# Two mixers: the products of a head's outputs grouped by kind, and attention's products ordered by tile before head

## The chip, the core and the metric

The kernel runs on one core of a Trainium2 chip, in float32. The metric is the device time of one execution in microseconds (us): the median of three runs is 1829.69 us (1829.17 to 1829.71).

## What is computed

512 tokens of width 1024 go through two blocks. The first is a mixer (a gated linear recurrence called hgrn2 beside a spatial gate), a mixture of 32 experts and a small per-layer embedding. The second is a mixer (stick-breaking attention beside gated linear attention) and an MLP. The change touches the recurrence of the first mixer and the attention of the second:

```python
def hgrn2_branch(q, f_raw, i_in, og, lb, norm_g):        # 4 heads, key and value 128 wide
    C = HG_CHUNK                                         # 64 tokens, 8 chunks
    ...
    att = jnp.einsum('bcthk,bcshk->bchts', q_dec, k_inv)
    att = jnp.where(mask, att, jnp.zeros_like(att))
    o_intra = jnp.einsum('bchts,bcshv->bcthv', att, v)
    dS = jnp.einsum('bcshk,bcshv->bchkv', k_end, v)
    ...                                                  # S = decay * S + dS, from chunk to chunk
    o_inter = jnp.einsum('bcthk,cbhkv->bcthv', q_dec, s_starts)
    o = (o_intra + o_inter).reshape(B, S, HG_HEADS, HG_VAL)
    o = o * lax.rsqrt(jnp.mean(o * o, axis=-1, keepdims=True) + EPS)
    ...

def stick_breaking_attention(q, k, v):                   # 8 heads of 64
    for start in range(0, s_len, Q_BLOCK):
        ...
        z = jnp.einsum('bhtd,bhsd->bhts', q[:, :, start:end], kb) * scale
        log_beta = jax.nn.log_sigmoid(z)
        log_fail = jnp.where(past, log_beta - z, 0.0)
        later = lax.cumsum(log_fail, axis=3, reverse=True) - log_fail
        w = jnp.where(past, jnp.exp(log_beta + later), 0.0)
        outs.append(jnp.einsum('bhts,bhsd->bhtd', w, vb))
```

## The kernel before

Every engine has an instruction list of its own; a scheduler decides the order of the lists from the order of the code, its priorities and the free buffers, and semaphores join them. So an edit of one loop can move other instructions too. The big projections go through `acc` rows (lines 268 to 270): a weight block is split into a high and a low part (`whi` on ACT, line 165; `wlo` on DVE, line 167), and each 128x512 output takes 24 matmuls.

**hgrn** (line 462 on) works on two heads at a time (`hp`), each head `m` of the pair in this order. Scores `pat` (line 581) are 8 products, one for each chunk of 64 tokens; DVE masks them into `att` (line 583). The states' increments `pds` (line 591) are 7 products of 64 rows, chunk c reading the array's half `i = c % 2` and writing one of two banks; DVE adds them up into the states `hS` (lines 597 and 600). The outputs `po` are 15 products in one bank: for each chunk the product of `att` and the values (line 608, 64 rows by 64 columns) and, from the second chunk on, the product of the decayed query and the state before it (line 611, 128 rows by 64 columns), one behind the other. Even chunks write the lower 64 partitions of `po`, odd ones the upper. ACT squares `po`, GpSimd takes the root (`hst`), DVE scales (`hy`, line 623) and PE transposes the result into `pyb` (line 627). PSUM has 4 banks of kind `acc`, 2 of kind `tr` (transposes) and 2 of kind `m` (`misc`: `pat`, `pds`, `po`) here. The projection of the output gate (`proj_tm` with `eg`) stands behind the first head's outputs in the code.

**sticks** (line 1386 on) handles the 8 heads in 4 pairs, a pair on the two halves of 64 rows, and each pair in three groups of key tiles: tiles 2 and 3 together, tile 1, tile 0. For a group, PE computes the scores `z` (line 1464), 256 and 128 columns for each head in the first group, 384 in the second and 512 in the third. ACT and DVE make softplus values of them (`se`, `sp`), PE adds the running sums to the same banks (lines 1491 and 1494), ACT takes the exponent `sw` (line 1498), GpSimd masks it, and PE multiplies it by the values into `po` (line 1505; the code's `v` products, 64 output partitions for each head). Between the groups a fixed number of `acc` outputs, called fills (24 rows each), are called from the table `FILL`, 11 in all:

```python
FILL = ((1, 0, 1), (1, 0, 1), (1, 0, 1), (3, 1, 1))
        ctx.enter_context(N.banks(acc=1, po=1, pz=3))
```

With one `acc` bank a fill can't begin before ACT has copied out the one before (line 1400 for a query, line 1405 for a key).

Of the kernel before, what the change touches and what calls it, by code (L numbers as in the profile page):

```python
# [18 lines left out]
P = 128  # L19
T = 512  # L20
NT = T // P
# [440 lines left out]
def hgrn(N, a, w_in, hT, yb):  # L462
    nc = N.nc
    C = 64
    with N.pool("hg") as hg:
# [9 lines left out]
        att = []  # L475
# [49 lines left out]
        for hp in range(2):  # L525
            wf = N.wtile(w_in[:, 1536 + hp * 256:1536 + (hp + 1) * 256], KD, 256)
            k_, eb_, qd_, ki_, ke_ = [], [], [], [], []
            tables = N.exp_ln()
            for m in range(2):
                h = 2 * hp + m  # L530
                p = N.acc("pf")
                N.fm_acc(p, wf, m, hT, KD)

                k, s = N.tmp("hk"), N.tmp("hf")
                nc.vector.tensor_scalar(k, p, -87.0, None, op0=OP.max)
                with N.tc.issue_after(tables):
                    nc.scalar.activation(s, k, AF.Exp, scale=-1.0)
                l = N.tmp("hl")
                nc.scalar.activation(l, s, AF.Ln, bias=1.0)
                nc.scalar.activation(s, s, AF.Ln, bias=1.0, scale=lb[:, 20 + h:21 + h])  # L540
                nc.vector.tensor_tensor(s, s, l, op=OP.subtract)
                nc.vector.tensor_tensor(k, k, l, op=OP.add)
                nc.scalar.activation(k, k, AF.Exp, scale=-1.0)
                k1 = lb[:, 24 + h:25 + h]
                b = N.tmp("hb")
                nc.vector.tensor_tensor_scan(b, rst, s, 0.0, op0=OP.mult, op1=OP.add)
                eb = hg.tile([P, T], F32, tag="heb", bufs=2, name="heb")
                nc.scalar.activation(eb, b, AF.Exp)
                nb = N.tmp("hnb")
                nc.scalar.activation(nb, b, AF.Exp, scale=-1.0)  # L550
                ki = hg.tile([P, T], F32, tag="hki", bufs=2, name="hki")
                nc.vector.scalar_tensor_tensor(ki, k, k1, nb, op0=OP.mult, op1=OP.mult)
                b3 = b.rearrange("p (c t) -> p c t", t=C)
                d = N.tmp("hd")
                nc.vector.tensor_tensor(d.rearrange("p (c t) -> p c t", t=C), b3[:, :, C - 1:C].to_broadcast([P, 8, C]),
                                        b3, op=OP.subtract)
                nc.scalar.activation(d, d, AF.Exp)
                nc.vector.scalar_tensor_tensor(d, k, k1, d, op0=OP.mult, op1=OP.mult)
                pt = N.trp("pke")
                for t in range(NT):  # L560
                    nc.tensor.transpose(pt[:, t * P:(t + 1) * P], d[:, t * P:(t + 1) * P], N.ident)
                ke = hg.tile([P, T], F32, tag="hke", bufs=2, name="hke")
                nc.scalar.activation(ke, pt, AF.Copy)
                eb_.append(eb); ki_.append(ki); ke_.append(ke)
            wq = N.wtile(w_in[:, 1024 + hp * 256:1024 + (hp + 1) * 256], KD, 256)
            for m in range(2):
                p = N.acc("pq")
                N.fm_acc(p, wq, m, hT, KD)
                s = N.th1(p, "hq")
                nc.vector.scalar_tensor_tensor(s, s, 1.0, p, op0=OP.add, op1=OP.mult)  # L570
                qd = hg.tile([P, T], F32, tag="hqd", bufs=2, name="hqd")
                nc.vector.scalar_tensor_tensor(qd, s, 0.5, eb_[m], op0=OP.mult, op1=OP.mult)
                qd_.append(qd)

            for m in range(2):
                h = 2 * hp + m
                p = N.misc("pat")
                for j in range(NT):
                    for i in range(2):
                        c = slice((2 * j + i) * C, (2 * j + i + 1) * C)  # L580
                        nc.tensor.matmul(p[i * 64:(i + 1) * 64, j * C:(j + 1) * C], lhsT=ki_[m][:, c], rhs=qd_[m][:, c],
                                         start=True, stop=True)
                nc.vector.copy_predicated(att[m], cm[:, None, :].to_broadcast([P, 4, 64]),
                                          p[:, :256].rearrange("p (j t) -> p j t", j=4))

                S = hg.tile([P, 7, P], F32, tag="hS", bufs=2, name="hS")
                pd = [N.misc("pds0"), N.misc("pds1")]
                for c in range(7):
                    j, i = divmod(c, 2)
                    r = slice(i * 64, (i + 1) * 64)  # L590
                    nc.tensor.matmul(pd[i][:, j * P:(j + 1) * P], lhsT=ke_[m][r, j * P:(j + 1) * P],
                                     rhs=vv[r, j, h * P:(h + 1) * P], start=True, stop=True)
                for c in range(7):
                    j, i = divmod(c, 2)
                    dsl = pd[i][:, j * P:(j + 1) * P]
                    if c == 0:
                        nc.vector.tensor_copy(S[:, 0, :], dsl)
                    else:
                        e = (c + 1) * C - 1
                        nc.vector.scalar_tensor_tensor(S[:, c, :], S[:, c - 1, :], eb_[m][:, e:e + 1], dsl,  # L600
                                                       op0=OP.mult, op1=OP.add)
                po = N.misc("po")
                for j in range(NT):
                    for i in range(2):
                        c = 2 * j + i
                        r = slice(i * 64, (i + 1) * 64)
                        o = po[r, j * P:(j + 1) * P]
                        nc.tensor.matmul(o, lhsT=att[m][r, j, :], rhs=vv[r, j, h * P:(h + 1) * P],
                                         start=True, stop=(c == 0))
                        if c > 0:  # L610
                            nc.tensor.matmul(o, lhsT=qd_[m][:, c * C:(c + 1) * C], rhs=S[:, c - 1, :],
                                             start=False, stop=True)
                st = hg.tile([P, 12], F32, tag="hst", bufs=4, name="hst")
                jk = hg.tile([P, P], F32, tag="jk2", bufs=2, name="jk2")
                for j in range(NT):
                    nc.scalar.activation(jk, po[:, j * P:(j + 1) * P], AF.Square, accum_out=st[:, j:j + 1])
                nc.vector.tensor_scalar(st[:, 4:8], st[:, 0:4], 1.0 / P, EPS, op0=OP.mult, op1=OP.add)
                N.rpow(st[:, 8:12], st[:, 4:8])
                if hp == 0 and m == 0:
                    N.proj_tm(w_in, 2560, hT, eg)  # L620
                y = hg.tile([P, NT, P], F32, tag="hy", bufs=2, name="hy")
                for j in range(NT):
                    nc.vector.scalar_tensor_tensor(y[:, j, :], po[:, j * P:(j + 1) * P], st[:, 8 + j:9 + j],
                                                   G[:, j, h * P:(h + 1) * P], op0=OP.mult, op1=OP.mult)
                pt = N.trp("pyb")
                for j in range(NT):
                    nc.tensor.transpose(pt[:, j * P:(j + 1) * P], y[:, j, :], N.ident)
                N.split(yb[0][:, h, :], yb[1][:, h, :], pt)
# [757 lines left out]
def sticks(N, a, w_in, hT, osb, gv, low, fq, bk, lead):  # L1386
# [3 lines left out]
    with N.pool("sb") as sb, ExitStack() as ctx:  # L1390
# [63 lines left out]
        def pair(c):  # L1454
            po = prev = None
            for tiles in ((2, 3), (1,), (0,)):
# [1 line left out]
                nd, n = len(tiles), sum(T - i * P for i in tiles)  # L1458
                n0 = T - tiles[0] * P
                z = N.bank("pz", "pz", 2)[:, :, :n]  # L1460
                for h in range(2):
                    r, c0 = slice(h * 64, (h + 1) * 64), 0
                    for i in tiles:
                        nc.tensor.matmul(z[:, h, c0:c0 + T - i * P], lhsT=k[c][r, i * P:(i + 1) * P], rhs=q[c][r, i * P:],
                                         start=c0 == 0, stop=True, skip_group_check=True)
                        c0 += T - i * P
                e = sb.tile([P, 2, T], F32, tag="se", bufs=3, name="se")[:, :, :n]
                nc.scalar.activation(e, z, AF.Abs)
# [20 lines left out]
                for h in range(2):  # L1489
# [3 lines left out]
                    for x in range(2):  # L1493
# [4 lines left out]
                nc.scalar.activation(w, z, AF.Exp)  # L1498
                nc.gpsimd.affine_select(diag(w), diag(w), pattern=[[0, 2], [0, nd], [1, P]] if nd == 2 else [[0, 2], [1, P]],
                                        compare_op=OP.is_gt, fill=0.0, base=0, channel_multiplier=-1)  # L1500
                for h in range(2):
                    c1 = n
                    for i in reversed(tiles):
                        c0 = c1 - (T - i * P)
                        nc.tensor.matmul(po[h * 64:(h + 1) * 64, i * P:],  # L1505
                                         lhsT=v[:, i, (2 * c + h) * 64:(2 * c + h + 1) * 64], rhs=w[:, h, c0:c1],
                                         start=(i == NT - 1), stop=(i == 0), skip_group_check=True)
                        c1 = c0
                prev = e[:, :, :n0]
                for _ in range(FILL[c][tiles[0]]):  # L1510
                    next(fill, 0)
# [262 lines left out]
```

## Time and profile before

| what | value |
|---|---|
| median of three runs | 1829.69 us |
| profiled execution | 1830.18 us, of which the span of its instructions is 1828.5 us |
| mean granted TensorE clock | 0.999 of full speed |
| busy | PE 98%, DVE 47%, ACT 32%, POOL 4% of the span |
| first mixer's recurrence | about 60 to 160 us of the span |
| experts' weights arriving at the highest rate | about 410 to 870 us |
| second mixer's attention | about 980 to 1092 us |

PE is TensorE's matmuls, DVE is VectorE, ACT is ScalarE, POOL is GpSimd. A float32 matmul of two plain operands shows as two passes, so 8 such products are a row "x16". In a row of the timeline the first number is the start, the second the time from the first start to the modelled end of the last instruction in it; the next row often starts some 0.07 us before that end, since matmuls are pipelined.

### The profile page before, as it was taken

What the parts mean: (1) busy time and instruction counts of PE and PEld (TensorE: products, weight loads), DVE (VectorE), ACT (ScalarE), POOL (GpSimd) and SP (SyncE); (2) the same over time, 40 slices, a digit from 0 to 9 for tenths busy, and PEclk for the clock granted to TensorE, in tenths of its full rate; (3) what the DMA queues carried; (4) which work ended last, traced back from release to release, by engine and by line L of the source; (5) the groups of instructions that cost most, each with busy time, mean ns of one, the idle gap of its engine ahead of it and who ended that gap; (6) DMA issues with size and microseconds to landing.
All of it is one profiled execution on the core that took longest, in us unless ns stands there. A gap on an engine that the chain in (4) does not pass through costs nothing.

```text
span 1828.5 us, 20908 instructions
## 1 busy us (share of the span) xinstructions
PE 1793.8 (98%) x8425; PEld 1240.1 (68%) x8425; DVE 857.1 (47%) x1620; ACT 586.7 (32%) x953; POOL 76.0 (4%) x136
## 2 busy tenths in 40 slices
PE   7999999999999999999999999999999999999998
PEld 5777888864443444443677668787888888888886
DVE  6565433365545445324764557555224443333333
ACT  6453322322111112111755652424223432222221
POOL 1001000100000000000020010000000000000000
PEclk9999999999999999999999999999999999999999
DMA  5122223979999997999312021212233222332221
GB/s 191 47 92 90 78 93 97 354 258 424 423 423 423 423 409 303 424 423 374 131 36 91 24 73 46 92 36 81 82 103 130 87 72 94 96 104 99 92 92 46
DMA packets 117888, 322.60 MB, mean 176 GB/s; under 512 B 8797, under 2 KB 69393, under 8 KB 93720
## 3 DMA queue, kind: packets, MB, share of 16 engines
q1 hardware_dynamic: 115192, 315.46, 45.7%
q0 software_dynamic: 2016, 3.64, 0.5%
q10 hardware_dynamic: 576, 2.10, 0.3%
q8 instruction: 68, 1.11, 0.3%
q14 instruction: 36, 0.29, 0.0%
HBM read 320.68 MB, written 4.19 MB: 178 GB/s over the span
## 4 chain that ended last, share of the span: by engine, by line
PE 46%; issue 3%; ACT 2%; DVE 1%; POOL 1%; DMA 0%; POOLq 0%; DVEq 0%; ACTq 0%
PE acc L268 7%; PE acc L269 7%; PE acc L270 7%; PE pf L270 3%; PE pf L269 3%; PE pf L268 3%; PE pg L270 2%; PE pg L268 2%; PE pg L269 2%; PE psc L1605 2%; PE pu L270 1%; PE pu L268 1%; PE pu L269 1%; PE pa L1090 1%; PE po L1505 1%
## 5 line engine op out<-in xcount | busy, mean ns | idle before, releaser
L167 DVE TENSOR_TENSOR wlo<-wraw,whi 128x1024 fp32r<-128x1024 f32 (+2 forms) x165 | 226.5, 1384 | 350.9 <-PE pg L269 107.6
L165 ACT ACTIVATE whi<-wraw 128x1024 fp32r<-128x1024 f32 (+2 forms) x169 | 193.3, 1165 | 246.6 <-DMA wraw<-in_w_ff_dram 121.4
L268 PE MATMUL acc<-wh,whi 128*128 128x512 f32 (+1 forms) x448 | 170.7, 381 | 1.7 <-ACT fq L1442 1.0
L269 PE MATMUL acc<-wh,whi 128*128 128x512 f32 (+1 forms) x448 | 170.4, 380 | 0.0
L270 PE MATMUL acc<-wh,wlo 128*128 128x512 f32 (+1 forms) x448 | 169.9, 379 | 0.0
L268 PE MATMUL acc<-whi,wh 128*128 128x512 f32 x288 | 116.2, 404 | 0.6 <-ACT wh L165 0.4
L270 PE MATMUL acc<-whi,wh 128*128 128x512 f32 x288 | 114.9, 401 | 0.9 <-DVE wh L169 0.9
L269 PE MATMUL acc<-wlo,wh 128*128 128x512 f32 x288 | 114.9, 400 | 0.2 <-POOL wlo L167 0.2
L269 PE MATMUL pg<-wh,whi 128*128 128x512 f32 x256 | 101.5, 397 | 0.0
L268 PE MATMUL pg<-wh,whi 128*128 128x512 f32 x256 | 101.3, 396 | 0.0
L270 PE MATMUL pg<-wh,wlo 128*128 128x512 f32 x256 | 101.1, 395 | 0.0
L268 PE MATMUL pf<-whi,jh 128*128 128x512 f32 x256 | 101.1, 395 | 0.0
L269 PE MATMUL pf<-wlo,jh 128*128 128x512 f32 x256 | 101.1, 395 | 0.0
L270 PE MATMUL pf<-whi,jl 128*128 128x512 f32 x256 | 101.1, 395 | 0.0
L268 PEld LDWEIGHTS acc<-wh,whi 128*128 128x128 f32 x448 | 84.5, 189 | 21.5 <-issue 1.5
L269 PEld LDWEIGHTS acc<-wh,whi 128*128 128x128 f32 x448 | 84.5, 189 | 18.0 <-issue 1.8
L270 PEld LDWEIGHTS acc<-wh,wlo 128*128 128x128 f32 x448 | 84.5, 189 | 16.5
L1104 DVE TENSOR_TENSOR X<-pc,X 128x512 f32<-128x512 f32 x128 | 80.6, 684 | 15.2 <-PE pc L1102 14.3
L1090 PE MATMUL pa<-ww,wm 128*64 128x512 f32 x176 | 80.8, 599 | 0.3 <-PEq L803 0.3
L1091 PE MATMUL pa<-ww,wm 128*64 128x512 f32 x168 | 77.3, 599 | 0.0
L1102 PEld LDWEIGHTS pc<-y,OT 128*128 128x128 f32 x256 | 44.6, 188 | 41.7 <-issue 24.1
L1102 PE MATMUL pc<-y,OT 128*128 128x512 f32 x256 | 71.0, 411 | 0.3 <-DVE X L1104 0.2
(472 smaller groups left out, 3454.5 us busy)
## 6 DMA issues: line engine op xcount, KB each, us to landing
ww<-in_w_dram SPq DMA_DIRECT2D x71, 1024.0 KB
wraw<-in_w_in_dram SPq DMA_DIRECT2D x44, 1024.0 KB
wr<-in_w_dram SPq DMA_DIRECT2D x34, 1024.0 KB
wm<-in_w_dram SPq DMA_DIRECT2D x33, 1024.0 KB
wraw<-in_w_ff_dram SPq DMA_DIRECT2D x32, 1024.0 KB
wh<-in_w_dram SPq DMA_DIRECT2D x31, 1024.0 KB
we<-in_w_dram SPq DMA_DIRECT2D x23, 1024.0 KB
wraw<-in_w_out_dram SPq DMA_DIRECT2D x8, 1024.0 KB
```

The lines of the kernel that those rows point to most:

```text
L165: nc.scalar.activation(hi, src, AF.Copy, scale=scale)
L167: (pool or nc.vector).tensor_tensor(lo, src, f32v(hi), op=OP.subtract)
L268: mm(out, lhsT=lh, rhs=rh, start=start, stop=False, **kw)
L269: mm(out, lhsT=lh, rhs=rl, start=False, stop=False, **kw)
L270: mm(out, lhsT=ll, rhs=rh, start=False, stop=stop, **kw)
L1090: nc.tensor.matmul(p[0:64], lhsT=x.xT[:, kk, :64], rhs=wt[0][:, k, :], start=kk == 0, stop=kk == 7)
L1091: x.ups.append(nc.tensor.matmul(p[64:128], lhsT=x.xT[:, kk, 64:], rhs=wt[1][:, k, :], start=kk == 0, stop=kk == 7).ins)
L1102: nc.tensor.matmul(pc, lhsT=OT[:, t * P:(t + 1) * P], rhs=y[i], start=i == 0, stop=i == 1)
L1104: nc.vector.tensor_tensor(x, pc, x, op=OP.add)
L1505: nc.tensor.matmul(po[h * 64:(h + 1) * 64, i * P:], lhsT=v[:, i, (2 * c + h) * 64:(2 * c + h + 1) * 64], rhs=w[:, h, c0:c1], start=(i == N ...
L1605: nc.tensor.matmul(pl[:, cs], lhsT=fk[:, m, cs], rhs=fq[:, m, cs], start=True, stop=True)
```

## The change

In hgrn the scores `pat` go to a bank of kind `tr`. The states of both heads of a pair are computed ahead of the outputs of either. The output gate's projection stands between the two (for the first pair). A head's outputs are now all 8 products of `att` first and then all 7 products of the states, each kind going from one half to the other. In sticks the loops of the `z` products are exchanged (tile outside, head inside) and given a high priority; the loops of the `v` products are exchanged too. The number of instructions on each engine stays the same.

```diff
@@ hgrn, first mixer, for a pair of heads hp @@
+            S_ = []
             for m in range(2):
                 h = 2 * hp + m
-                p = N.misc("pat")
+                p = N.trp("pat")
...
                 S = hg.tile([P, 7, P], F32, tag="hS", bufs=2, name="hS")
+                S_.append(S)
                 pd = [N.misc("pds0"), N.misc("pds1")]
...
+            if hp == 0:
+                N.proj_tm(w_in, 2560, hT, eg)
+            for m in range(2):
+                h, S = 2 * hp + m, S_[m]
+
                 po = N.misc("po")
-                for j in range(NT):
-                    for i in range(2):
-                        c = 2 * j + i
-                        r = slice(i * 64, (i + 1) * 64)
-                        o = po[r, j * P:(j + 1) * P]
-                        nc.tensor.matmul(o, lhsT=att[m][r, j, :], rhs=vv[r, j, h * P:(h + 1) * P],
-                                         start=True, stop=(c == 0))
-                        if c > 0:
-                            nc.tensor.matmul(o, lhsT=qd_[m][:, c * C:(c + 1) * C], rhs=S[:, c - 1, :],
-                                             start=False, stop=True)
+                for s in range(2):
+                    for j in range(NT):
+                        for i in range(2):
+                            c = 2 * j + i
+                            r = slice(i * 64, (i + 1) * 64)
+                            o = po[r, j * P:(j + 1) * P]
+                            if s == 0:
+                                nc.tensor.matmul(o, lhsT=att[m][r, j, :], rhs=vv[r, j, h * P:(h + 1) * P],
+                                                 start=j == 0, stop=c == 0, skip_group_check=True)
+                            elif c > 0:
+                                nc.tensor.matmul(o, lhsT=qd_[m][:, c * C:(c + 1) * C], rhs=S[:, c - 1, :],
+                                                 start=False, stop=True, skip_group_check=True)
...
-                if hp == 0 and m == 0:
-                    N.proj_tm(w_in, 2560, hT, eg)
@@ sticks, second mixer, for a pair of heads c @@
-                for h in range(2):
-                    r, c0 = slice(h * 64, (h + 1) * 64), 0
+                c0 = 0
+                with N.tc.high_priority():
                     for i in tiles:
-                        nc.tensor.matmul(z[:, h, c0:c0 + T - i * P], lhsT=k[c][r, i * P:(i + 1) * P], rhs=q[c][r, i * P:],
-                                         start=c0 == 0, stop=True, skip_group_check=True)
+                        for h in range(2):
+                            r = slice(h * 64, (h + 1) * 64)
+                            nc.tensor.matmul(z[:, h, c0:c0 + T - i * P], lhsT=k[c][r, i * P:(i + 1) * P],
+                                             rhs=q[c][r, i * P:], start=c0 == 0, stop=True, skip_group_check=True)
                         c0 += T - i * P
...
-                for h in range(2):
-                    c1 = n
-                    for i in reversed(tiles):
-                        c0 = c1 - (T - i * P)
+                c1 = n
+                for i in reversed(tiles):
+                    c0 = c1 - (T - i * P)
+                    for h in range(2):
                         nc.tensor.matmul(po[h * 64:(h + 1) * 64, i * P:],
                                          lhsT=v[:, i, (2 * c + h) * 64:(2 * c + h + 1) * 64], rhs=w[:, h, c0:c1],
                                          start=(i == NT - 1), stop=(i == 0), skip_group_check=True)
-                        c1 = c0
+                    c1 = c0
```

The lines of the changed kernel stand 2 to 9 further down: `pds` is line 593 there, the `po` products of hgrn are lines 617 and 620, `z` is line 1473, the `v` product line 1514, and ACT's Abs, Exp, Ln and `sw` are lines 1477, 1478, 1479 and 1507.

**First place: hgrn on PE.** The increments `pds` of the third head (the first of the second pair); the number behind `pds` is the tile, 1039 for the even chunks on the lower half of the array's rows, 1040 for the odd ones on the upper half. Before:

```order
L591 MATMUL pds_1039<-hv,hke 128x128 x4
L269 MATMUL acc<-wlo,wh_68 128x512
L270 MATMUL acc<-whi,wh_68 128x512
L268 MATMUL acc<-whi,wh_69 128x512
L269 MATMUL acc<-wlo,wh_69 128x512
L270 MATMUL acc<-whi,wh_69 128x512
L268 MATMUL acc<-whi,wh_69 128x512
L269 MATMUL acc<-wlo,wh_69 128x512
L270 MATMUL acc<-whi,wh_69 128x512
L268 MATMUL acc<-whi,wh_70 128x512
L591 MATMUL pds_1040<-hv,hke 128x128 x3
```

And of the change, for the same head:

```order
L593 MATMUL pds_1039<-hv,hke 128x128
L593 MATMUL pds_1040<-hv,hke 128x128
L593 MATMUL pds_1039<-hv,hke 128x128
L593 MATMUL pds_1040<-hv,hke 128x128
L593 MATMUL pds_1039<-hv,hke 128x128
L593 MATMUL pds_1040<-hv,hke 128x128
L593 MATMUL pds_1039<-hv,hke 128x128
```

The seven products now stand together and go from half to half; all four heads' seven stand together, the second's and the fourth's in the order even, even, odd, odd, even, odd, even. Before, the first head's stood together as three even, three odd, one even, the second head's were cut into even, even and odd, odd, even, odd, even, and the fourth's were cut like the third's above.

The outputs `po` of the first head (`att_119` holds its masked scores, `att_121` those of the second). Before:

```order
L608 MATMUL po<-hv,att_119 64x128 x2
L611 MATMUL po<-hS,hqd 64x128
L608 MATMUL po<-hv,att_119 64x128
L611 MATMUL po<-hS,hqd 64x128
L608 MATMUL po<-hv,att_119 64x128
L611 MATMUL po<-hS,hqd 64x128
L608 MATMUL po<-hv,att_119 64x128
L611 MATMUL po<-hS,hqd 64x128
```

And of the change, with the rows on either side:

```order
L269 MATMUL acc<-wlo,wh_71 128x512
L270 MATMUL acc<-whi,wh_71 128x512
L617 MATMUL po<-hv,att_119 64x128 x8
L620 MATMUL po<-hS,hqd 64x128 x7
L617 MATMUL po<-hv,att_121 64x128 x8
L620 MATMUL po<-hS,hqd 64x128 x7
L268 MATMUL pf<-wh_68,whi 128x512
L269 MATMUL pf<-wh_68,whi 128x512
```

The two kinds no longer take turns, and the second head's outputs follow the first's, where projections, `pat` and `pds` of the next head stood between them.

**Second place: PE in the attention, at the first `z` group of the second pair** (256 and 128 columns for each head). Before, from the first of them on:

```order
L1464 MATMUL pz<-sq,sk 128x256
L1491 MATMUL pz<-sp,tri 128x384
L1494 MATMUL pz<-sr,one 128x256 x2
L1491 MATMUL pz<-sp,tri 128x384 x2
L1494 MATMUL pz<-sr,one 128x256 x2
L1464 MATMUL pz<-sq,sk 128x128
L1464 MATMUL pz<-sq,sk 128x256
L1491 MATMUL pz<-sp,tri 128x512
L1464 MATMUL pz<-sq,sk 128x128
L268 MATMUL acc<-wh_9409,whi 128x512
```

And of the change:

```order
L269 MATMUL acc<-wh_9410,whi 128x512
L270 MATMUL acc<-wh_9410,wlo 128x512
L1473 MATMUL pz<-sq,sk 128x256 x2
L1473 MATMUL pz<-sq,sk 128x128 x2
L1514 MATMUL po<-sw,sv 64x128 x2
L1514 MATMUL po<-sw,sv 64x256 x2
L1503 MATMUL pz<-sr,one 128x256
```

The four products stood in three pieces with other pairs' sums between them, the heads on either side of a gap. Now they are one piece, head beside head. The third and the fourth pair's were cut in the same way before and are one piece now; a `z` of 384 columns of the second pair and those of 512 columns of the first and the fourth had their two heads apart and have them together now.

**Third place: the beginning of the attention.** PE starts it in the change with all three groups of the first pair:

```order
L270 MATMUL acc<-wh_9412,wlo 128x512
L1473 MATMUL pz<-sq,sk 128x256
L1473 MATMUL pz<-sq,sk 128x384
L1473 MATMUL pz<-sq,sk 128x512
L1473 MATMUL pz<-sq,sk 128x384
L1473 MATMUL pz<-sq,sk 128x512
L1473 MATMUL pz<-sq,sk 128x256
L1473 MATMUL pz<-sq,sk 128x128 x2
L268 MATMUL acc<-wh_9409,whi 128x512
L269 MATMUL acc<-wh_9409,whi 128x512
```

Before, only the first group (256 and 128 columns) stood here; the second and third came 24 `acc` rows later. After these rows both versions have the 24 rows of the first fill. On ACT, from the table load at this place on, before:

```order
L1514 ACT_TABLE_LOAD
L165 ACTIVATE whi<-wraw 128x1024
L1468 ACTIVATE se<-pz 128x2x384
L165 ACTIVATE whi<-wraw 128x1024
L1469 ACTIVATE se<-se 128x2x384
L1470 ACTIVATE se<-se 128x2x384
L1400 ACTIVATE sq<-acc 128x512
L165 ACTIVATE sp<-se 128x2x384
L165 ACTIVATE whi<-wraw 128x1024
```

And of the change:

```order
L1523 ACT_TABLE_LOAD
L165 ACTIVATE whi<-wraw 128x1024 x2
L1477 ACTIVATE se<-pz 128x2x384 x2
L1478 ACTIVATE se<-se 128x2x384 x2
L1479 ACTIVATE se<-se 128x2x384 x2
L1477 ACTIVATE se<-pz 128x1024
L165 ACTIVATE whi<-wraw 128x1024
L1407 ACTIVATE sq<-acc 128x512
L165 ACTIVATE sp<-se 128x2x384 x2
```

The copy of the first fill, `sq<-acc`, stood behind one group's Abs, Exp and Ln; now it stands behind those of two groups and the Abs of the third, and behind one `whi` more.

## Rows read from the trace of the kernel before

**Rows 1.** Stretches of the span, from:to, length, busy PE, PEld, DVE, ACT, POOL, clock, DMA share, GB/s.

```profile
60.00:160.00 100.00, 97.85 (x537) 70.92 (x536) 50.75 (x91) 38.96 (x74) 4.19 (x5) 1.00 0.17 57
980.00:1092.00 112.00, 106.94 (x479) 71.36 (x478) 63.45 (x91) 73.90 (x90) 10.16 (x22) 1.00 0.17 54
400.00:600.00 200.00, 200.00 (x1011) 85.84 (x1009) 99.33 (x293) 31.19 (x63) 10.63 (x9) 1.00 1.01 418
```

**Rows 2.** Timeline of PE, first head's outputs in hgrn, their beginning and end.

```profile
73.55 0.44 PE L608 MATMUL po<-hv,att 64*64 64x128 f32 x4
73.92 0.43 PE L611 MATMUL po<-hS,hqd 128*64 128x128 f32 x2
...
78.25 0.43 PE L611 MATMUL po<-hS,hqd 128*64 128x128 f32 x2
78.61 0.50 PE L270 MATMUL acc<-whi,wh 128*128 128x512 f32 x1
```

**Rows 3.** Timeline of PE, scores and increments of hgrn's heads.

```profile
66.05 0.63 PE L561 MATMUL pke<-ident,hd 128*128 128x128 f32 x4 [0.19 <-DVE hd L558]
...
68.00 0.69 PE L581 MATMUL pat<-hqd,hki 128*64 128x64 f32 x16
68.62 1.55 PE L591 MATMUL pds<-hv,hke 64*128 64x128 f32 x14
70.09 0.50 PE L268 MATMUL acc<-whi,wh 128*128 128x512 f32 x1
...
95.06 0.71 PE L591 MATMUL pds<-hv,hke 64*128 64x128 f32 x4
...
95.95 0.93 PE L591 MATMUL pds<-hv,hke 64*128 64x128 f32 x10
...
127.55 1.16 PE L591 MATMUL pds<-hv,hke 64*128 64x128 f32 x8
...
130.93 0.93 PE L591 MATMUL pds<-hv,hke 64*128 64x128 f32 x6
```

**Rows 4.** Waits of PE from 55 to 180 us: total us, times, longest.

```profile
PE pyb L627 <- DVE hy L623: 2.0, 3, 0.8
```

**Rows 5.** Timeline of PE in the attention: `z` (L1464) and `v` products (L1505).

```profile
982.52 0.93 PE L1464 MATMUL pz<-sq,sk 64*128 64x256 f32 x8 [0.69 <-ACT sk L1405]
983.38 0.50 PE L268 MATMUL acc<-wh,whi 128*128 128x512 f32 x1
...
996.48 0.88 PE L1505 MATMUL po<-sw,sv 128*64 128x128 f32 x8 [0.65 <-POOL sw L1499]
...
1014.78 0.91 PE L1464 MATMUL pz<-sq,sk 64*128 64x384 f32 x2
...
1025.97 0.70 PE L1464 MATMUL pz<-sq,sk 64*128 64x256 f32 x2
...
1027.42 0.70 PE L1464 MATMUL pz<-sq,sk 64*128 64x128 f32 x4
...
1028.47 0.48 PE L1464 MATMUL pz<-sq,sk 64*128 64x128 f32 x2
...
1070.33 1.12 PE L1464 MATMUL pz<-sq,sk 64*128 64x512 f32 x2
```

**Rows 6.** Timeline of ACT at the beginning of the attention.

```profile
982.49 1.28 ACT L1514 ACT_TABLE_LOAD   x1
983.78 1.06 ACT L165 ACTIVATE whi<-wraw 128x1024 fp32r<-128x1024 f32 x1
984.75 0.80 ACT L1468 ACTIVATE se<-pz 128x768 f32<-128x768 f32 x1
...
986.39 0.84 ACT L1469 ACTIVATE se<-se 128x768 f32<-128x768 f32 x1
...
989.26 0.60 ACT L1400 ACTIVATE sq<-acc 128x512 f32<-128x512 f32 x1 [1.16 <-PE acc L270]
...
994.00 1.02 ACT L1468 ACTIVATE se<-pz 128x1024 f32<-128x1024 f32 x1
```

## Prediction

> **What bounds the kernel now.** I read the busy shares first, then the two stretches that the change touches, then PE's rows there, then what PE waits for. PE, TensorE's matmuls, is busy for 98% of the span (the table above), and in the two stretches still for 97.85 of 100 us and 106.94 of 112 us, while no other engine passes 73.90 of 112 [rows 1]. So the time is the length of PE's list plus its few gaps. The gaps are 2.15 us in the recurrence and 5.06 us in the attention. A shorter list on PE is shorter time, unless a gap opens. The reader is to see in [rows 2] that a busy PE can still be badly used: the outputs of one head run from 73.55 to 78.61, 5.06 us for 15 small products. They go in 14 groups, (78.61 - 73.55) / 14 = 0.36 us each. The first group holds two products, one on each half, and takes 0.37 like the others (73.55 to 73.92). A group costs 0.36 whatever is in it, because each changes the kind of product: from 64 rows to 128, and back.
>
> **hgrn, the outputs.** What is the price of such products in a run of one kind? The nearest row is a piece of four `pds` products, eight passes, all on one half of the array: the row says 1.16, and 0.07 of it lies under the next row, so 1.09 [rows 3]. The piece of three takes 0.86, so a further product on the same half adds 0.23. In a run of 8 `att` products four lie on each half. If the halves work side by side, the run costs 1.09, and the 7 state products (four and three) cost 1.09 too: 2.18 in place of 5.06. That is 2.88 a head and **11.5 us** for four heads. If the halves take turns instead, 8 products cost 1.09 + 4 x 0.23 = 2.01 and 7 cost 1.78, together 3.79: 1.27 a head, 5.1 in all. I take the first, because the first group of [rows 2] shows two products on two halves of one bank in 0.37, what a group of one costs, and because `pat` puts 16 passes, alternating, into 68.62 - 68.00 = 0.62 [rows 3].
>
> The Trainium skill speaks against a part of this. Its page "TensorEngine Tiling (Array Packing)", section "Gotcha 1: PSUM Pressure", says that different row tiles cannot access the same PSUM bank simultaneously, and the `att` products of the two halves are two row tiles that write one bank. By that rule the `att` run would take 2.01 where I count 1.09, and the gain would be 4 x 0.92 = 3.7 us smaller; the first group of rows 2, two such products in 0.37, speaks against the rule here, but it is only one pair of products.
>
> **hgrn, the increments.** Less the 0.07 each, the pieces of `pds` take 1.48 for the first head, 0.64 + 0.86 = 1.50 for the second, and 1.09 + 0.86 = 1.95 for the third; the fourth is cut like the third, so 1.95 [rows 3]. Together 6.88. In the change each head's seven are one alternating piece; at 1.09 each (again the price of four on one half) that is 4.36, **2.5 us** less. That order matters is in the rows: seven as three even, three odd, one even took 1.48, while five with the halves mixed (95.95) took 0.86, as long as three on one half. If the second and fourth head, which start with two of one half and two of the other, keep 1.5, the gain is 1.7.
>
> **hgrn, the gaps.** The rest of this edit moves work without changing its amount: the gate's projection, and `pat` in another bank. What covers the chain from a head's outputs over ACT, GpSimd and DVE to `pyb` is the `acc` and `pf` rows behind it. Before, PE waited three times there, 0.8 at the longest and 2.0 in all [rows 4], and 0.2 for a `pke` [rows 3]. In the change both heads of a pair finish their outputs at once, and ACT, GpSimd and DVE serve them one after the other, so that each of four groups of `pyb` may wait. I price each at the longest seen: 3.2. Each pair's second `pke` waits for DVE's `hd`, which nothing makes sooner, while the pieces ahead of it on PE get shorter: 0.8 again for each, 1.6. So 4.8 against 2.2, **2.6 us more**, with bounds of nothing (the projections cover all) and 5 (every wait twice as long). hgrn gives -11.5 - 2.5 + 2.6 = **-11.4**.
>
> **Attention, the z products.** A whole group of 256 and 128 columns for two heads costs 0.86 (982.52 to 983.38). The same group in three pieces costs 0.63 + 0.63 + 0.41 = 1.67 (the rows at 1025.97, 1027.42 and 1028.47, less 0.07 each) [rows 5]. Three pairs were cut like that: 3 x 0.81 = 2.4. A lone half of 384 columns costs 0.84 and a lone half of 512 costs 1.05, and beside the other head's half it would cost nothing; one of each, in the second and the fourth pair: 1.9. The first pair saves another lone half of 512, but its new list has three products of one head (256, 384, 512) before the first of the other. If the others can't start until the third has begun, 256 and 384 columns run alone, some 0.43 + 0.64 = 1.07 (lone rows less 0.2 for the change of kind), and the saving is gone. The `pds` of the first head, three even ahead of three odd, speak for that; the 0.86 of the group at 982.52, whose four products were listed head by head, against it. I take 0.4. Sum: **4.7 us** (4.3 to 5.4).
>
> **Attention, the v products.** The first group was listed as two products of one head and two of the other. It takes 0.88, no longer than the 0.91 of a single head's 384 columns in `z`, though each head has 384 columns [rows 5]. The halves already worked side by side, so exchanging the loops gives **nothing**; I see no loss in it either. One weight transfer for the gated linear attention is issued two places later on SP; the DMA engines are busy for 0.17 of this stretch [rows 1], so I count nothing for it.
>
> **Attention, the gaps.** With one `acc` bank the second fill waits until ACT has copied the first. Before, that copy began at 989.26, as PE finished, 5.9 us after the fill's first row [rows 5, 6]. In the change PE's first `z` groups take up to 2.3 + 1.07 = 3.4 us, so the fill begins at 985.9 and ends at 991.8. ACT has after the table load (to 983.78) two `whi` of about 1.0 (to 985.8), then needs the last products of the first group (985.9): two Abs of 0.80, two Exp of 0.84, two Ln of like length make 5.0 (990.9), the third group's Abs 1.02 (991.9), one more `whi` (992.9), the copy 0.6: 993.5 [rows 6]. PE waits 993.5 - 991.8 = **1.7 us**, where it waited for nothing before. What is queued behind on PE is all of the second fill and the sums of the first pair; ACT's `sp` stands right behind the copy, so those sums are late by as much. The other gaps stay as they are, 5.06 in all. Bounds: nothing, if the fill and ACT meet, and 5, if two later copies are late like this. Attention gives -4.7 + 1.7 = **-3.0**.
>
> **Sum.** -11.4 - 3.0 = -14.4 on the profiled execution's 1830.18 (span 1828.5 and 1.68 around it): 1815.8. The median of the runs shown is 0.49 below that execution, so **1815.3 us**.
>
> **Rivals.**
> - *The attention gives nothing*: two or three copies late by 1.7 eat the 4.7 of `z`. For it: one bank, and an ACT list that now bunches the work of two groups. Against: ACT is idle for a third of the stretch [rows 1]. Time 1818.3 to 1820.
> - *The halves take turns in one bank*: only for the `att` runs, 1815.3 + 3.7 = 1819.0; for both kinds 1821.7. Against: the 0.37 of the first group [rows 2]. This is the rule of the skill's page, with the chance below.
> - *Slower*: in the single `acc` bank every one of the 11 fills is copied out late by the three ACT steps of a group (0.80 + 0.84 + 0.84 = 2.5) that move ahead of it through the high priority: 27 us, and 1815.3 - 1.7 + 27.5 = 1841. The change's gain without gaps in the attention is 16.1, so it decides from the seventh fill on. Against: 73.90 of 112 us on ACT leave room [rows 1], and only the first copy stands visibly further back.
> - *The experts swallow the gain*: in 400 to 600 us the transfers take their engines' whole time (1.01, 418 GB/s) while PE is busy for 200 of 200 [rows 1]. If their start doesn't move with PE, the recurrence's 11.4 become a wait there: 1826.7. Against: buffers that PE's own rows free start those transfers, so they move along.
> - *More gain*: the new gaps don't come (4.3) and the first pair of the attention overlaps fully (0.7): 1810.3.
>
> **How the numbers follow.** Forecast 0.60, with its own range of 1811 to 1819 (the bounds of gaps and `pds`). Attention nothing 0.15; halves in turns 0.10; slower 0.03; experts 0.04; more gain 0.08. The range reaches down to 1809 and up to 1821.5, which leaves out about 0.15. A measurement of this kernel tells 0.2%, 3.7 us, from no change: below 1826.0 is faster. Only the slower rival and the most of the experts' lie above: faster 0.94, same 0.03, slower 0.03.
>
> **What would show it.** Right: the `po` rows of a head in two groups of about 1.1 us; the four `pds` each in one row near 1.1; `z` of 256 and 128 columns in one row of 0.9 for every pair; a wait of PE for `sq` near 992 us of about 2 us; the same offset of some 11 us from the experts' first row to their last. Wrong: an `att` run of 2 us; waits of PE on ACT's copies at more than two fills; waits on `pyb` or `pke` of more than 5 us together; weights that arrive too late for PE behind 400 us.

## The result and the profile after

The changed kernel takes 1808.86 us (median of 4 runs, 1808.56 to 1809.47), beside 1829.70 before: 20.8 us less, a ratio of 0.9888 with a 95% interval of 0.9873 to 0.9903. That is faster, as forecast, since the prediction counted anything below 1826.0 as faster. It lies below the forecast's own range of 1811 to 1819 and about 0.1 us below the low end of the wide one, 1809 to 1821.5; the forecast was 1815.3. The gain was 14.4 in the forecast and is 20.8. The nearest of the rivals is *more gain*, 1810.3 with a chance of 0.08.

The timeline of PE at the outputs of the first two heads, after (it answers to [rows 2]):

```profile
89.24 0.40 PE L270 MATMUL acc<-whi,wh 128*128 128x512 f32 x1
89.57 1.09 PE L617 MATMUL po<-hv,att 64*64 64x128 f32 x16
90.59 1.09 PE L620 MATMUL po<-hS,hqd 128*64 128x128 f32 x14
91.61 1.09 PE L617 MATMUL po<-hv,att 64*64 64x128 f32 x16
92.63 1.09 PE L620 MATMUL po<-hS,hqd 128*64 128x128 f32 x14
93.65 0.50 PE L268 MATMUL pf<-wh,whi 128*128 128x512 f32 x1
93.98 0.39 PE L269 MATMUL pf<-wh,whi 128*128 128x512 f32 x1
94.22 0.39 PE L270 MATMUL pf<-wh,wlo 128*128 128x512 f32 x1
...
98.22 0.33 PE L634 MATMUL pyb<-ident,hy 128*128 128x128 f32 x1 [0.35 <-DVE hy L630]
```

Each run of one kind takes 1.02 us from its start to the next row's, so a head takes 2.04 where it took 5.06. Of the two runs the first holds 8 products and the second 7, and they cost the same: what counts is four products on the fuller half. The rows behind show what a change of kind costs `acc` and `pf`: the first `pf` row takes 0.33 to the next start, the second 0.24.

The timeline of PE at the increments and transposes after (to [rows 3]), and its waits in the recurrence (55 to 180 us, to [rows 4]):

```profile
61.92 1.16 PE L593 MATMUL pds<-hv,hke 64*128 64x128 f32 x14
...
65.65 0.63 PE L561 MATMUL pke<-ident,hd 128*128 128x128 f32 x4 [0.52 <-DVE hd L558]
...
67.60 0.69 PE L582 MATMUL pat<-hqd,hki 128*64 128x64 f32 x16
68.22 0.49 PE L270 MATMUL acc<-whi,wh 128*128 128x512 f32 x1
68.64 0.69 PE L582 MATMUL pat<-hqd,hki 128*64 128x64 f32 x16
...
71.78 1.16 PE L593 MATMUL pds<-hv,hke 64*128 64x128 f32 x14
```

```profile
PE pke L561 <- DVE hd L558: 1.2, 2, 0.7
PE pyb L634 <- DVE hy L630: 1.1, 3, 0.4
```

All seven increments of a head take 1.16 - 0.07 = 1.09, in both orders (even and odd in turns, and even, even, odd, odd, even, odd, even). The waits are 2.3 in all, where they were 2.2 ([rows 3, 4]). The rows between a head's outputs and its first transpose, before (fourth head) and after (third head, whose outputs end at 133.99, where the fourth head's begin):

```profile
152.98 0.50 PE L268 MATMUL acc<-whi,wh 128*128 128x512 f32 x1
...
156.39 0.33 PE L627 MATMUL pyb<-ident,hy 128*128 128x128 f32 x1 [0.82 <-DVE hy L623]
```

```profile
133.99 1.09 PE L617 MATMUL po<-hv,att 64*64 64x128 f32 x16
135.01 1.09 PE L620 MATMUL po<-hS,hqd 128*64 128x128 f32 x14
...
137.40 0.59 PE L634 MATMUL pyb<-ident,hy 128*128 128x128 f32 x2 [0.40 <-DVE hy L630]
```

Both times it is 3.41 us from the end of the outputs to the transpose.

The timeline of PE at the attention's beginning and at the second pair (to [rows 5]):

```profile
968.55 2.96 PE L1473 MATMUL pz<-sq,sk 64*128 64x256 f32 x16 [0.69 <-ACT sk L1412]
...
978.54 0.50 PE L268 MATMUL acc<-wh,whi 128*128 128x512 f32 x1 [1.25 <-ACT sq L1407]
...
982.70 0.92 PE L1473 MATMUL pz<-sq,sk 64*128 64x256 f32 x8
983.63 0.87 PE L1514 MATMUL po<-sw,sv 128*64 128x128 f32 x8
...
986.48 0.92 PE L1473 MATMUL pz<-sq,sk 64*128 64x384 f32 x4
...
991.50 1.13 PE L1473 MATMUL pz<-sq,sk 64*128 64x512 f32 x4
...
1069.68 0.50 PE L268 MATMUL acc<-wh,whi 128*128 128x512 f32 x1 [0.69 <-ACT fq L1449]
```

And PE's waits there (960 to 1100 us):

```profile
PE acc L268 <- ACT sq L1407: 1.3, 1, 1.3
PE po L1514 <- POOL sw L1508: 0.8, 2, 0.5
PE pz L1473 <- ACT sk L1412: 0.7, 1, 0.7
PE acc L268 <- ACT fq L1449: 0.7, 1, 0.7
PE acc L268 <- ACT low L1443: 0.7, 1, 0.7
```

Before, the row that waits for the last `fq`, and three of PE's waits in the same stretch, were:

```profile
1090.42 0.50 PE L268 MATMUL acc<-wh,whi 128*128 128x512 f32 x1 [1.02 <-ACT fq L1442]
```

```profile
PE po L1505 <- POOL sw L1499: 1.3, 2, 0.7
PE pz L1491 <- ACT sp L165: 1.3, 2, 0.6
PE acc L268 <- ACT fq L1442: 1.0, 1, 1.0
```

The attention begins at 968.55 in place of 982.52, 13.97 earlier, which is the recurrence's gain as it comes through the experts. From there to the row that waits for the last `fq` it takes 101.13 us; before, that row stood at 1090.42, 107.90 after the first `z`. So the attention itself gives 6.8. The wait for the copy of the first fill is there, 1.25.

### The profile page after: what moved, and what is told of

The parts are those of the page before. It is cut to its first block, busy times and chain, and to the rows that moved or that the text cites. A ratio compares the mean times of both kernels' runs of the same rounds, so it can differ in the third digit from the quotient of the medians.

```text
span 1807.7 us, 20918 instructions
## 1 busy us (share of the span) xinstructions
PE 1773.9 (98%) x8425; PEld 1232.3 (68%) x8425; DVE 857.4 (47%) x1620; ACT 584.3 (32%) x953; POOL 79.7 (4%) x136
## 4 chain that ended last, share of the span: by engine, by line
PE 50%; ACT 2%; DVE 1%; issue 1%; POOL 1%; DVEq 0%; POOLq 0%; ACTq 0%
PE acc L268 8%; PE acc L270 8%; PE acc L269 8%; PE pf L270 3%; PE pf L268 3%; PE pf L269 3%; PE pg L270 2%; PE pg L268 2%; PE pg L269 2%; PE psc L1614 2%; PE pu L270 1%; PE pu L268 1%; PE pu L269 1%; PE pa L1097 1%; PE py L1186 1%
```

## The experiments

Ratios are to the kernel before, with 95% intervals. The changed kernel once more, beside the last of the experiments:

> The changed kernel once more, beside the one before on the same chip, to compare: 1808.9 within 0.5.

Measured: 1808.41 us, 0.9890 (0.9873 to 0.9906). The two medians of this kernel lie 0.45 apart, and those of the kernel before, taken beside the different experiments, between 1829.06 and 1829.70. So a difference of half a microsecond is not told from none.

**The two edits apart.** First hgrn's edit alone, the attention being that of before:

```diff
 # sticks as before the change
+            S_ = []
...
+            if hp == 0:
+                N.proj_tm(w_in, 2560, hT, eg)
...
+                for s in range(2):
...
```

> The recurrence's edit alone, attention as before. Theory (the two edits are worth what their own rows show, and add up): outputs 4 x 3.02 and increments 2.5 and no more waiting on PE, 14.5 us less in the recurrence, of which some 0.9 are lost again in the experts: 1829.7 - 13.6 = 1816. The attention's rows stand as in [rows 5]. Rival (a part of the attention's gain comes from the earlier or different arrival of the first mixer's work): 1811 to 1813.

Measured: 1815.67 us, 0.9927 (0.9913 to 0.9940). Then the attention's edit alone, with the `v` loops exchanged too:

```diff
 # hgrn as before the change
+                with N.tc.high_priority():
                     for i in tiles:
+                        for h in range(2):
...
```

> The attention's edit alone, the recurrence as before. Theory (the edits add up): about 6.5 us less, 1823. The rows of z in whole groups, one wait of about 1.3 us for the copy of the first fill. Rival (the gain of the attention needs the other edit): 1826 or more, and correspondingly less in the other kernel.

Measured: 1823.59 us, 0.9966 (0.9952 to 0.9980). The gains are 13.9 and 6.0, 19.9 together, and 20.7 to 20.8 in the change. They add up to within 0.9 us, which is hardly more than such medians leave open, and the experts in between pass the recurrence's gain on: their first `pc` row stands at 435.76 before and at 421.46 after, and at 968.22 with hgrn's edit alone the attention begins 14.30 earlier.

**Kinds in turns.** The outputs in the old order, everything else as changed:

```diff
-                for s in range(2):
-                    for j in range(NT):
-                        for i in range(2):
+                for j in range(NT):
+                    for i in range(2):
+                        for s in range(2):
...
-                                                 start=j == 0, stop=c == 0, skip_group_check=True)
+                                                 start=True, stop=c == 0, skip_group_check=True)
```

> The changed kernel, but the outputs of a head in the old order: for each chunk the product of the scores and then that of the state; everything else of the change stays, both heads' outputs stay together behind all states. Theory (a change of kind costs 0.36 us, a run of one kind 1.02): four heads x 3.02 = 12.1 us back, 1821. Rival (the gain is in taking the states of both heads ahead and in fewer visits of the projections in between): at most 4 back, 1809 to 1813.

Measured: 1820.32 us, 0.9951 (0.9936 to 0.9966), 11.5 to 11.9 more than the changed kernel. The rows of the timeline are again those of [rows 2]:

```profile
89.72 0.43 PE L617 MATMUL po<-hv,att 64*64 64x128 f32 x4
90.09 0.43 PE L620 MATMUL po<-hS,hqd 128*64 128x128 f32 x2
90.45 0.43 PE L617 MATMUL po<-hv,att 64*64 64x128 f32 x2
```

So of 13.9 us in the recurrence some 11.7 are the split by kind. The other 2.2 belong to the rest of that edit together; no run tries by itself what it is worth to take the states ahead of the outputs.

**Halves in sequence.** Within a run first the lower half's products, then the upper's:

```diff
                 for s in range(2):
-                    for j in range(NT):
-                        for i in range(2):
+                    for i in range(2):
+                        for j in range(NT):
```

> The changed kernel, but within a run of one kind first the four products of the lower half and then those of the upper. Theory (halves overlap only where neighbours in the list lie on different halves, as the 1.48 us of three even, three odd, one even increments says): a run takes some 1.6 us in place of 1.02, eight runs, 4 to 5 us back, 1813 to 1814. Rival (the order within a run doesn't matter, as the first v group's 0.88 us says, whose products are listed head by head): 1808.9.

Measured: 1810.95 us, 0.9898 (0.9883 to 0.9913), 2.1 to 2.5 more than the changed kernel: between the theories. The timeline:

```profile
89.59 1.58 PE L617 MATMUL po<-hv,att 64*64 64x128 f32 x16
91.10 1.36 PE L620 MATMUL po<-hS,hqd 128*64 128x128 f32 x14
92.39 1.58 PE L617 MATMUL po<-hv,att 64*64 64x128 f32 x16
```

A run of four and four takes 1.51, one of three and four 1.29, where turns take 1.02. So the halves' alternation is worth 0.49 and 0.27 of a run, 3.0 for four heads by the rows, and 2.1 to 2.5 came out in the time, in which PE also waits 0.3 less for `hy` (0.8 in place of 1.1); the greater part of the split's gain stays without it. The halves overlap partly even in this order: two halves one after the other would take about 2.0 by [rows 3].

**The scores in the old kind of bank.**

```diff
-                p = N.trp("pat")
+                p = N.misc("pat")
```

> The changed kernel with the scores pat back in a bank of kind m. The scheduler then lists every head's increments as three even, three odd, one even, behind pat. Theory (the bank of pat decides the order of the increments, and that order costs 1.48 against 1.09 us): 4 x 0.39 = 1.6 us back, 1810.4, and the four rows of increments at about 1.55. Rival (the increments' gain comes from standing together, whatever their order): 1808.9, or less if nearer increments shorten the waits.

Measured: 1808.9 us, 0.9885 (0.9870 to 0.9901). The time is the rival's, and the rows of the increments are the theory's. Timeline, and waits in the recurrence:

```profile
67.66 0.69 PE L582 MATMUL pat<-hqd,hki 128*64 128x64 f32 x16
68.27 1.55 PE L593 MATMUL pds<-hv,hke 64*128 64x128 f32 x14
```

```profile
PE pyb L634 <- DVE hy L630: 1.1, 3, 0.4
PE pke L561 <- DVE hd L558: 0.5, 2, 0.3
```

The increments take 1.48 in this order, 0.39 more for each of four heads (1.6). But PE waits 0.7 less for `pke`, and the increments follow `pat` directly, which saves the `acc` rows between the two that a change of kind makes longer: the one between two `pat` takes 0.42 in the changed kernel (68.22 to 68.64), where a row among its like takes 0.23. Counted above 0.233 us a row, all `acc`, `pf` and `pq` rows of the recurrence hold 0.8 us less of such lengthening here. Together that is nearly the 1.6. The better order of the increments is real in its rows, and the time shows nothing of it.

**No priority for z**, the loops staying exchanged:

```diff
-                with N.tc.high_priority():
+                with ExitStack():
```

> The changed kernel without the high priority of the z products; their loops stay exchanged. The scheduler lists them apart again: the last group of the first and fourth pair, the first group of the second, third and fourth, and the second pair's 384. Theory (the attention's gain is the priority's: whole groups): 4 to 6 us back, 1813 to 1815. Rival (the exchanged loops are what counts): 1808.9.

Measured: 1814.62 us, 0.9917 (0.9904 to 0.9931), 5.8 to 6.2 more than the changed kernel. The pieces are back in the timeline, and the waits of before with them (960 to 1100 us):

```profile
986.39 0.70 PE L1473 MATMUL pz<-sq,sk 64*128 64x256 f32 x2
...
988.20 0.70 PE L1473 MATMUL pz<-sq,sk 64*128 64x256 f32 x2
...
989.26 0.49 PE L1473 MATMUL pz<-sq,sk 64*128 64x128 f32 x4
```

```profile
PE po L1514 <- POOL sw L1508: 1.3, 2, 0.7
PE pz L1500 <- ACT sp L165: 1.2, 2, 0.6
PE acc L268 <- ACT fq L1449: 1.0, 1, 1.0
```

**Heads outside**, with the priority, in the `z` loops and the `v` loops:

```diff
-                    for i in tiles:
-                        for h in range(2):
...
+                    for h in range(2):
...
+                        for i in tiles:
...
-                for i in reversed(tiles):
...
-                    for h in range(2):
+                for h in range(2):
...
+                    for i in reversed(tiles):
...
```

> The changed kernel with the priority, but z's and v's loops as before: head outside, tile inside. Theory (order within a whole group of one or two products a head costs nothing): 1808.9, z groups of 256 and 128 at 0.93 and the first v groups at 0.88 as in [rows 5]. Rival (neighbours on different halves count here as in the recurrence): eight groups at about 0.3 more, 1811.

Measured: 1808.91 us, 0.9885 (0.9870 to 0.9900), the time and the rows of the theory:

```profile
982.65 0.93 PE L1472 MATMUL pz<-sq,sk 64*128 64x256 f32 x8
983.58 0.88 PE L1513 MATMUL po<-sw,sv 128*64 128x128 f32 x8
```

Both runs together say that the exchanged loops give nothing, and the priority nearly all of the attention's gain. The same holds without the priority: hgrn's edit alone (old loops) and the kernel without priority (exchanged loops) were 1.05 us apart in time, but from the first `z` row to the last `v` row they take 103.69 (968.22 to 1071.91) and 103.64 (968.03 to 1071.67), so that difference is not the loops'.

**The third group later.** The first pair's 512 columns without the priority:

```diff
-                with N.tc.high_priority():
+                with N.tc.high_priority() if c or tiles[0] else ExitStack():
```

> The changed kernel, but the first pair's third z group (512 columns) without the priority; it then stands behind the first fill, whole, and ACT copies that fill before the third group's Abs. Theory (three products of one head ahead of the other's first cost 0.6 us at the start, and the Abs of 1.0 us ahead of the copy the same in the wait): the first z row falls from 2.96 to about 1.75, the third group costs 1.05 later, the wait for the copy of 1.3 us is gone or small, but ACT reaches the second exponents later: 1807.8 to 1808.9. Rival (what is taken from this wait comes back in the waits for sp and sw behind it): 1808.9 to 1810.

Measured: 1808.71 us, 0.9884 (0.9868 to 0.9899), not told apart from the change. Timeline of PE:

```profile
968.33 1.57 PE L1473 MATMUL pz<-sq,sk 64*128 64x256 f32 x12 [0.69 <-ACT sk L1412]
975.62 1.13 PE L1473 MATMUL pz<-sq,sk 64*128 64x512 f32 x4
977.41 0.50 PE L268 MATMUL acc<-wh,whi 128*128 128x512 f32 x1 [0.65 <-ACT sq L1407]
979.09 0.44 PE L1500 MATMUL pz<-sp,tri 128*128 128x384 f32 x1 [0.48 <-ACT sp L165]
```

The groups come out as the theory has it (1.50 and 1.06 in place of 2.89). The wait for the first copy is halved, but a second copy is waited for as well (0.9 in all in place of 1.3), and a wait for `sp` of 0.48 is new, as the rival says: PE's waits in the attention are 4.2 as before this edit, and the time from the first `z` row to the last `v` row is 88.68 (968.33 to 1057.01) beside 88.67 (968.55 to 1057.22).

**The gate's projection back behind the first head's outputs.**

```diff
-            if hp == 0:
-                N.proj_tm(w_in, 2560, hT, eg)
             for m in range(2):
...
+                if hp == 0 and m == 0:
+                    N.proj_tm(w_in, 2560, hT, eg)
```

> The changed kernel with the output gate's projection back behind the first head's outputs, as before the change. The scheduler then puts 12 rows between the second head's increments and the first head's outputs, 59 rows between the two heads' outputs, and the first head's transposes ahead of the second head's outputs. Theory (moving work that costs the same moves only waits, and these are small while any projection rows cover the chains): the four runs of outputs stay at 1.02 each, waits of PE in the recurrence between 1.5 and 4 us against 2.3, 1808 to 1810.5. Rival (the projection's place is what keeps the new waits away, so that the 4.8 us of waits that I counted come back without it): 1811 to 1812.

Measured: 1808.06 us, 0.9883 (0.9866 to 0.9899), waits on `pyb` and `pke` 1.1 each, 2.2 in all. The projection's place neither makes nor hides a wait that the time would show. This edit and the one before it in one kernel:

> The changed kernel with the gate's projection behind the first head's outputs and the first pair's third z group without the priority. Theory (each alone measured within a us of the change, so together at most a us below it): 1807.5 to 1809, not told apart from the change. Rival (the two small gains are real and add up): 1807.0 to 1807.5, with the change itself at 1808.8 beside it.

Measured: 1809.11 us (1807.87 to 1810.31), 0.9894 (0.9877 to 0.9910), against 1808.41 for the change beside it. No version here beats the change by what can be measured.

## Why the prediction was right, and where it was too small

- **The outputs: right.** 11.5 forecast, 4 x (5.06 - 2.04) = 12.1 by the rows, and 11.5 to 11.9 when this alone is taken back. The halves work side by side in one bank: 16 passes in 1.02. The rival of halves in turns asked for 2.01 in the `att` run. The rule of the Trainium skill's page "TensorEngine Tiling (Array Packing)", "Gotcha 1: PSUM Pressure", by which the prediction has the `att` run at 2.01, does not show in this time; the trace, with its 1.02 in four runs of four, disagrees with it.
- **The increments: the rows right, their worth not.** 4 x 1.09 = 4.36 was forecast and is what stands there. The kernel with `pat` in the old kind of bank lists every head's as three, three and one, at 1.48, and takes the same time, so some 1.6 of these 2.5 us are given back, by its rows in waits for `hd` and in longer `acc` rows.
- **The gaps of the recurrence: the step that failed first.** "I price each at the longest seen" gave 4.8; 2.3 was measured. The covering rows were there. In the first pair 17 `pf` rows stand behind the outputs, 93.65 to 98.22, and the eight transposes then alternate with single `pf` rows, so PE waits 0.35 once. In the second pair it waits 0.40 and 0.34. There the chain from the end of a head's outputs to its first `pyb` is as long as it was before, 3.41 us (the rows are in the first section). But now the other head's outputs, 2.04, stand in front of it. So the order that the prediction feared brings cover of its own: three waits of 1.1 in all, not four of 0.8. Two `pke` at 0.8 were 1.2 in all. This is 2.5 us of the 6.4 that the forecast lacks.
- **z: right.** Forecast 4.7. The 18 pieces of before add up to 15.88 and the 10 of the changed kernel to 11.25 (each from its start to the next row's): 4.6. The first pair's list with three products of one head ahead takes 2.89, the middle of the 2.3 to 3.4 of the prediction, whose 0.4 lay between two rows that spoke against each other; the last section has what the trace shows of it.
- **v: right**, by the kernel with the heads outside.
- **The gaps of the attention: the second step that failed.** The wait for the first copy was forecast at 1.7 and is 1.25; its place and its chain are right. "The other gaps stay as they are, 5.06 in all" was wrong: the wait for `sp` (1.3) is gone, those for `sw` went from 1.3 to 0.8, that for `fq` from 1.0 to 0.7. Together the waits are 4.2 in place of the 6.8 of the forecast, another 2.6 us. The run without the priority brings all three back, so it is the early `z` that removes them. That they go because ACT has its work sooner is likely, and no row was read for it.
- **A term that I left out**: the rows around the `z` pieces. From the first `z` row to the wait for `fq`, all `acc` and `plow` rows (each from its start to the next row's, waits taken off) take 60.06 before and 59.26 after, and the sums on `pz` 17.23 and 16.80: 1.2 us less with the same number of rows. A part of it is seen: an `acc` row that follows `z` or `v` products takes 0.33, one that follows another `acc` row 0.23 and one that follows sums mostly 0.23 to 0.28, and there are 13 of the first sort before and 9 after, which is 0.4. The rest stays open, and no run tries the term by itself.
- **The sum.** More than forecast: 2.5 (waits in the recurrence), 2.6 (waits in the attention), 0.6 (outputs) and 1.2 (the term left out). Less than forecast: 0.1 (`z`) and 0.5, by which the 13.97 at the attention's beginning fall short of the 14.5 that the recurrence's terms make (12.1 + 2.5 - 0.1). Together 6.3, against 20.8 - 14.4 = 6.4. The 0.5 is no sure loss: the second run of the changed kernel begins the attention at 967.88, 14.64 earlier than the kernel before.
- **The rivals.** The experts pass on what they get: their `pc` rows begin 14.30 and end 13.93 earlier (from 884.50 to 870.57 for the last). The slower rival needed late copies at seven fills; one is late. *More gain* came true by half: the new gaps of the recurrence did not come, but the wait for the first copy did, and the first pair's `z` did not overlap fully.

## What to carry to other kernels

Put small products of different shapes on PE into runs of one kind: here a group behind a change of kind cost 0.36 us, whether it held one product or two, and a product in a run 0.13 (1.02 for 8). Read the cost of a piece by its start and the next row's start, and compare the same products whole and cut. A new wait on paper should be priced by its chain (3.41 here) less the rows that the new order puts in front of it, not by the longest wait of before; and when an operation is pulled ahead, the waits behind it are forecast anew and not carried over.

## What the runs showed of the hardware that was not expected

Products on two halves overlap across some distance in the list, not only between neighbours. Two products of one half ahead of the other half's cost nothing (0.93 against 0.92 for the first `z` group, listed by heads or by tiles, and 1.50 for the whole first row of the kernel with the third group later). Three ahead cost something in the three places that have them: the first `z` row took 2.89 where full overlap is worked out as 2.35 (the 1.50 and a lone 512 of 1.05 less 0.2 for the change of kind), the state runs with halves in sequence 1.29 against 1.02, and the increments 1.48 against 1.09. Four ahead cost 0.49 of a run of 1.02.

The single records of the kept traces, which the timeline merges into these rows, show where the second half joins. In the first `z` row the list is 256, 384 and 512 columns of one head and then 384 of the other. The 256 start at 968.55; both 384 start at 969.09, ahead of the 512 that are listed before one of them (969.73). So the 256 alone stood by themselves, for 0.54 us, and 2.35 + 0.54 is the 2.89. With halves in sequence the second half joins as the third of four products begins (89.60, then 90.09), and as the second of three (91.10, then 91.38). In these places the second half began when two of the products listed ahead of it were left, the one just beginning included, and the time lost is the time until then. The increments do not fit: there the second half joined after 0.61 (68.62, then 69.23), when the third of three products had begun. Why stays open; no run was made for it.
